# A gated delta rule among projection products: the silu clamp on another engine, scan steps at other distances, and one product with ones

## The chip, the cores and the metric

The kernel runs on one core of one Trainium2 chip. The metric is the device time of one execution in microseconds, the median of several runs. A core has five engines that work side by side and wait for each other through semaphores: TensorE (PE in the profile, its weight loads PEld), VectorE (DVE), ScalarE (ACT), GpSimd (POOL) and SyncE (SP, which issues most of the DMAs here). Each engine takes its own instructions in a fixed order.

## The reference

The trunk has two layers, each with a mixer and a SwiGLU channel mixer, and ends with a modulated RMSNorm. It is applied to two groups, 512 and 256 tokens wide, with shared weights. The kernel keeps both side by side, 768 tokens, with features on the 128 partitions. The first layer mixes with a Fourier transform. The second is the bidirectional gated delta rule with 8 heads of width 128, and all of the change lies in it:

```python
def gdn_mixer(h, w_in, conv_w, a_log, dt_bias, norm_g, w_out):
    proj = h @ w_in
    qkv = silu(centred_depthwise_conv(proj[..., :GDN_QKV_DIM], conv_w))     # 5 taps
    z = ...; ab = ...                                                       # the rest of proj
    q = l2norm(q) * (GDN_HEAD_DIM ** -0.5)
    k = l2norm(k)
    g = -exp(a_log) * softplus(ab[:, :, 0:2] + dt_bias)
    beta = sigmoid(ab[:, :, 2:4])
    o_fwd = gated_delta_chunked(q, k, v, g[:, :, 0], beta[:, :, 0])
    o_bwd = gated_delta_chunked(q[:, ::-1], k[:, ::-1], v[:, ::-1], ...)[:, ::-1]
    o = o_fwd + o_bwd
    o = o * rsqrt(mean(o * o) + EPS) * norm_g * silu(z)
    return o @ w_out
...
    # gated_delta_chunked, per chunk: a triangular system, then a scan over the chunks
    sol = triangular_solve(I + strict(kb @ k.T * decay), [v * beta, kb * exp(gc)])
    def step(state, xs):
        delta = u_i - w_i @ state
        o = qd_i @ state + qk_i @ delta
        state = state * gl_i + kd_i.T @ delta
```

## The kernel before

**The whole.** First the Fourier layer with its channel mixer, then the delta stage, then the second channel mixer and the final norm. Large products are done in three passes with operands split into a high and a low part (hh and hl for the activations, wh and wl for the weights; `split_w`, lines 147 to 153, casts on ScalarE and subtracts on DVE).

**A head.** `prepare` (line 811) runs for the 8 heads in turn. It makes four projection products, for k, q, v and z, each over 8 chunks of the input features for the 512-token segment and then for the 256-token segment, 3 passes each, so 48 matmuls a product (`product`, line 188). k, q and v go through `conv_block` (line 756): ScalarE evicts the product into `pad` and a scaled copy into `wa`, DVE adds four taps to it (line 768), and then comes a silu. It is made from exponentials so that ScalarE keeps one table: `silu_factor` (line 712) clamps its input at -44 on GpSimd (line 713) and does Exp, Ln with bias 1 and Exp on ScalarE (lines 714 to 716); DVE multiplies the factor in (lines 772, 773). z gets the same factor (line 866).

**Placed steps.** Beside its products a head has smaller steps, which are placed among the products by a plan written out by hand. After each chunk of a product `tick` (line 732) adds 0.421 x 3 x its width to a counter `now`, which is 647 for a 512-wide chunk and 323 for a 256-wide one; 7760 for a product and 31040 for a head. Whatever is due by then is traced at that place, inside `issue_after`, which ties its TensorE instructions behind the chunk's last matmul (`run_next`, line 727). A step of the other engines is not tied, and a scheduler that orders each engine's queue by its own estimate of when an instruction is ready has the last word, so a step can stand later than its place. `PLACES` (line 57) gives five places counted from the head's start: the norm of k, the k-by-k product and the solver (`chunk_kk`, which also stores the matrix to DRAM for it), the decayed q, the k-by-q product, and the transposed v. `SCAN` (line 58) is where the scan of the head begins. `HOPS` (line 56) has the distances between the steps of the scan.

**The solver** (line 870) inverts the 16 by 16 diagonal blocks: the matrix goes to DRAM (`atd`) and comes back as lanes (`uu`), some 30 small DVE operations follow, and the result goes by DRAM (`solved`) into `cc`. GpSimd prepares the masked matrix `am` (line 897).

**The scan** (lines 899 and 946) first builds the full inverse in three levels of 16, 32 and 64. At a level, in the names used below, T are the transposes of `cc` (line 915; masked by DVE at line 917), Z the product with `am` (copied out by ScalarE at line 929), and R the product that updates `cc` on DVE (line 939) or, at level 64, is copied into `rr` by ScalarE (lines 942, 943). So T16 needs the solver's `cc`, and R64 needs the copy of Z64. Distances: HOPS[0] ahead of T32 and T64, HOPS[1] from T to Z, HOPS[2] from Z to R. Then come four steps over the token chunks, in both directions at once: pk (the state with k; DVE makes `xx`, line 975), py (`xx` with `rr`; ScalarE makes `yk` and `yy`), pu (`yk` with k; DVE makes the state `st`, line 992), at distances HOPS[3], [4] and [5]. The first step has no pk and the last no pu; the steps are numbered 0 to 3. After HOPS[6] the output products follow (lines 995 to 1006), and after HOPS[7] the norm: ones times the squares of q, and ones times the squares of the output, summed in PSUM (lines 1017, 1018), then Ln and Exp on ScalarE and two products on DVE; the result goes to DRAM (`ogd`), for the last head straight into hh and hl.

**Order of heads.** The scan of a head starts in the next head's products. After the last head all that is due for head 6 is run at once (line 1032), the results are loaded back from `ogd`, and seven output products over heads 0 to 6 carry the scan of head 7. Most buffers of the scan exist once (`rr`, `yy`, `xx`, `am`, `st`), those of a head twice (`kT`, `qd`, `pm`, `cc`, `zs`), and three PSUM banks `sm` serve all of the scan's products.

Of the kernel before, what the change touches and what calls it, by code (L numbers as in the profile page):

```python
# [15 lines left out]
ALU = mybir.AluOpType  # L16
# [36 lines left out]
LANES = NT * P // BASE  # L53
LSTEP = BASE * (P + 1)
NEGBIG = -1e30
HOPS = (1150.0, 1080.0, 1150.0, 1130.0, 830.0, 2080.0, 1150.0, 720.0)
PLACES = (16100.0, 20200.0, 22900.0, 29400.0, 36200.0)
SCAN = 35100.0

_TAB = {}  # L60

# [48 lines left out]
def encoder_kernel(  # L110
# [5 lines left out]
    V, A_, G = nc.vector, nc.scalar, nc.gpsimd  # L116
# [7 lines left out]
    ones = const.tile([P, P], F32, name="ones")  # L124
# [6 lines left out]
    def mm(out, lhsT, rhs, start=True, stop=True, **kw):  # L131
        return nc.tensor.matmul(out, lhsT, rhs, start=start, stop=stop, **kw)  # L132
# [31 lines left out]
    def load_block(w2d, k0, kc, m0):  # L164
        stg = fetch(w2d, k0, kc, m0)
        ah, al = [], []
        step = kc if kc <= HK else (kc + 1) // 2
        for a in range(0, kc, step):
            n = min(step, kc - a)
            wh, wl = split_w(stg[:, a : a + n])  # L170
            ah += [wh[:, k] for k in range(n)]
            al += [wl[:, k] for k in range(n)]
        return ah, al
# [14 lines left out]
    def product(pool, w, ah, al, kc, tick=None):  # L188
        out = []
        for g, (lo, ln) in enumerate(SEGS):  # L190
            ps = bank(pool, g)[:, :ln]
            for last in passes(ps, w, [a[:, lo : lo + ln] for a in ah[:kc]], [a[:, lo : lo + ln] for a in al[:kc]]):
                if tick:
                    tick(ln * 3 * 0.421, last)
            out.append(ps)
        return out
# [283 lines left out]
    with ExitStack() as l0:  # L480
# [8 lines left out]
        with ExitStack() as fs:  # L489
# [41 lines left out]
            for c in range(KC):  # L531
                pcs.append(fp.tile([P, NC + NS], F32, name="xt", bufs=8))
                ps = pbig.tile([P, 1024], F32, name="big")
                oc, os_ = 0, 512
                for g, s in ((0, S0), (1, S1)):
                    for par in (0, 1):
# [3 lines left out]
                        for kt in range(nkt):  # L540
                            o, n = COLS[f"seq{g}_{kt}_{par}"]
                            src = (odd if par else even)[2 if g else kt][:, c * P : (c + 1) * P]
# [71 lines left out]
    with ExitStack() as gs:  # L614
# [16 lines left out]
        def work(name="wa", bufs=2):  # L631
            return ga.tile([P, T + 2], F32, name=name, bufs=bufs)
# [76 lines left out]
        o16 = COLS["eye16"][0] - FCOLS  # L709
        eye16 = gtab[:LANES, o16 : o16 + BASE * BASE]  # L710

        def silu_factor(e, src, eng):
            eng.tensor_scalar(e, src, -44.0, None, ALU.max)  # L713
            A_.activation(e, e, AF.Exp, scale=-1.0)  # L714
            A_.activation(e, e, AF.Ln, bias=1.0)
            A_.activation(e, e, AF.Exp, scale=-1.0)
# [39 lines left out]
        def conv_block(h, which, pool, tag, bufs):  # L756
            wb = load_block(win, 0, KC, which * D + h * P)
            pq = product(ppr, wb, hh, hl, KC, tick)
            wc = [cwT[:, d * 24 + which * 8 + h : d * 24 + which * 8 + h + 1] for d in range(5)]
            acc = work()  # L760
            with tc.high_priority():
                A_.copy(pad[:, 2 : 2 + S0], pq[0])
                A_.copy(pad[:, S0 + 4 : T + 4], pq[1])
                A_.activation(acc[:, :S0], pq[0], AF.Copy, scale=wc[2])
                A_.activation(acc[:, S0 + 2 :], pq[1], AF.Copy, scale=wc[2])  # L765
            G.memset(acc[:, S0 : S0 + 2], 0.0)
            for d in (0, 1, 3, 4):
                V.scalar_tensor_tensor(acc, pad[:, d : d + T + 2], wc[d], acc, ALU.mult, ALU.add)  # L768
            e = work("we")
            silu_factor(e, acc, G)  # L770
            out = pool.tile(head_shape, F32, name=tag, bufs=bufs)
            V.tensor_tensor(out[:, :S0], acc[:, :S0], e[:, :S0], ALU.mult)
            V.tensor_tensor(out[:, S0:], acc[:, S0 + 2 :], e[:, S0 + 2 :], ALU.mult)
            return out
# [33 lines left out]
        def both(ap, n=NT):  # L808
            return ap.unsqueeze(1).to_broadcast([P, 2, n, P])

        def prepare(h):
            def col(t, d, j):
                return t[:, j, d * 8 + h : d * 8 + h + 1]

            raw = raws[h]
            base = line["now"]
            kT = conv_block(h, 1, gp, "kT", 2)
            qd = gp.tile([P, 2, NT, P], F32, name="qd", bufs=2)
            A_.activation(qd, raw, AF.Exp)
            pm = gp.tile([P, 2, NT, P], F32, name="pm", bufs=2)  # L820
            for d in range(2):
                G.affine_select(pm[:, d], raw[:, d], pattern=[[0, NT], [1 - 2 * d, P]], compare_op=ALU.is_ge, fill=NEGBIG,
                                base=0, channel_multiplier=2 * d - 1)
                for j in range(NT):
                    A_.activation(pm[:, d, j], pm[:, d, j], AF.Exp, bias=col(ngml, d, j))
            at = gp.tile([P, NT, P], F32, name="at", bufs=2)
            V.tensor_tensor(at, pm[:, 0], pm[:, 1], ALU.add)
            out = {"pm": pm, "qd": qd, "at": at, "kT": kT}

            def norm_k():  # L830
                rs = feat_norm(kT, work()[:, :T], work("we")[:, :T])
                V.tensor_tensor(kT, kT, rs, ALU.mult)

            def chunk_kk():
                pairwise(kT, kT, lambda b0, ps: V.tensor_tensor(at[:, b0 : b0 + NB], ps, at[:, b0 : b0 + NB], ALU.mult))
                atd = dgp.tile([NT * UN], F32, name="atd")
                nc.sync.dma_start(dram_full(atd), at)
                out["cc"] = solve(h, atd)
                siblings(out, LEVELS[0])
                out["kk"] = token_major(kT, "kk")  # L840

            def decay_q():
                V.tensor_tensor(qd, qd, both(tiles6(qT)), ALU.mult)

            def chunk_kq():
                pairwise(kT, qT, lambda b0, ps: V.tensor_tensor(pm[:, :, b0 : b0 + NB], both(ps, NB), pm[:, :, b0 : b0 + NB], ALU.mult))

            def values():
                out["vk"] = token_major(vT, "vk")

            for t, fn in zip(PLACES, (norm_k, chunk_kk, decay_q, chunk_kq, values)):
                at_time(base + t, fn)
            at_time(base + SCAN, run(scan(h, out)))
            qT = conv_block(h, 0, ga, "qT", 2)
            out["qT"] = qT
            if h < H - 1:
                raws.append(fetch_gc(h + 1))
            vT = conv_block(h, 2, ga, "vT", 1)
            wb = load_block(win, 0, KC, 3 * D + h * P)
            pz = product(ppr, wb, hh, hl, KC, tick)  # L860
            e = work("we")[:, :T]
            zs = gp.tile([P, T], F32, name="zs", bufs=2)
            with tc.high_priority():
                for g, (lo, ln) in enumerate(SEGS):
                    A_.copy(zs[:, lo : lo + ln], pz[g])
            silu_factor(e, zs, G)
            V.tensor_tensor(zs, e, zs, ALU.mult)
            out["zs"] = zs

# [29 lines left out]
        def invert(src):  # L899
# [4 lines left out]
            for lv in LEVELS:  # L904
# [4 lines left out]
                if lv != LEVELS[0]:  # L909
                    yield HOPS[0]  # L910
                t1 = {}
# [6 lines left out]
                if lv == LEVELS[-1]:  # L918
                    for d in range(2):
                        G.affine_select(rr[:, d], cc, pattern=[[0, NT], [1 - 2 * d, P]], compare_op=ALU.is_ge, fill=0.0,  # L920
                                        base=0, channel_multiplier=2 * d - 1)
                yield HOPS[1]
                zz = {}
# [6 lines left out]
                if lv != LEVELS[-1]:  # L930
                    siblings(src, 2 * lv)
                yield HOPS[2]
                for b0 in halves:
# [12 lines left out]
        def scan(h, src):  # L946
# [5 lines left out]
            vk, zs = src["vk"], src["zs"]  # L952
# [5 lines left out]
            for stp in range(4):  # L958
# [11 lines left out]
                if stp:  # L970
                    yield HOPS[3]
                    pk = group(lambda d, j: kT[:, j * P : (j + 1) * P], lambda i: st[:, first - 4 + i], len(live))
# [4 lines left out]
                else:  # L977
                    xin = lambda i: vk[:, live[i][1]]
                yield HOPS[4]
                py = group(lambda d, j: rr[:, d, j], xin, len(live))  # L980
# [4 lines left out]
                if more:  # L985
                    yield HOPS[5]
                    pu = group(lambda d, j: kk[:, j], lambda i: yk[:, i], more)
# [21 lines left out]
            sq = gp.tile([P, 2 * NT, P], F32, name="yy")  # L1009
            so, sq = sq[:, :NT].rearrange(flat), sq[:, NT:].rearrange(flat)  # L1010
            A_.activation(sq, src["qT"], AF.Square, scale=P * math.sqrt(EPS))
            A_.activation(so, ob, AF.Square)
            yield HOPS[7]
            rs = gp.tile([P, 2, NT, P], F32, name="rr")[:, 0].rearrange(flat)
            for lo, ln in SEGS:
                ps = psm.tile([P, 512], F32, name="sm")
                mm(ps[:, :ln], ones, sq[:, lo : lo + ln], stop=False)
                mm(ps[:, :ln], ones, so[:, lo : lo + ln], start=False)
                A_.activation(rs[:, lo : lo + ln], ps[:, :ln], AF.Ln, bias=epsq, scale=1.0 / P)
            A_.activation(rs, rs, AF.Exp, scale=-0.5)  # L1020
            V.scalar_tensor_tensor(ob, ob, gT[:, 48:49], rs, ALU.mult, ALU.mult)
# [148 lines left out]
```

## Time and profile before

| | us |
|---|---|
| median of 3 runs | 1996.56 (1994.72 to 2004.65) |
| the profiled execution | 2001.88 |
| its span, first to last instruction | 2000.10 |
| PE busy in the span | 1877.7 |
| DVE busy | 1229.2 |
| ACT busy | 894.4 |
| POOL busy | 468.0 |
| delta stage, from k of head 0 to the last output product | about 770 to 1410 |

The profile is one execution. Its rows give an instruction's engine, line, operation and tiles (out<-in), with start and length in us; a square bracket at the end gives the idle time ahead of it and who ended it. Waits are put down to the instruction that came last by semaphore, which is not always the one that was really late. Most matmuls have line 132, since one helper issues them; they are told apart by their tiles. A matmul's length in a row is its latency: the next one starts before it ends, so the spacing of starts is what it holds the engine for. An f32 product counts as two passes in the rows.

### The profile page before, as it was taken

How to read it: one execution, taken by the hardware profiler on the slowest of the kernel's cores; microseconds unless marked ns; L12 is line 12 of the kernel's file. 1: busy time of each engine (PE TensorE's matmuls, PEld its weight loads, DVE VectorE, ACT ScalarE, POOL GpSimd, SP SyncE). 2: the span in 40 equal slices, each digit the busy share in tenths (PEclk: the TensorE clock that was granted, in tenths of full speed). 3: DMA queues.
4: the chain of work that ended last, by engine and by line, in shares of the span. 5: the costliest groups of instructions: out<-in, count | busy, mean ns of one | idle time of the engine just before them, and what ended most of it. 6: DMA issues, size and time to landing. Idle time of an engine off the chain costs nothing.

```text
span 2000.1 us, 29707 instructions
## 1 busy us (share of the span) xinstructions
PE 1877.7 (94%) x11529; PEld 1657.3 (83%) x11529; DVE 1229.2 (61%) x2009; ACT 894.4 (45%) x1712; POOL 468.0 (23%) x370
## 2 busy tenths in 40 slices
PE   8898999999999999889898898889789999999998
PEld 6585989989798987778777777778579998999998
DVE  4637645545454657877686677664685565656565
ACT  3525524424142446655655656543454352524243
POOL 1314202111111101243333332320341211111231
PEclk9999999999999999999999999989889999999999
DMA  7654234453533144211121221141122222222211
GB/s 261 212 179 137 77 108 138 132 185 118 183 116 117 55 130 125 73 48 49 54 74 41 62 66 47 50 144 38 51 55 57 74 70 64 69 78 74 62 55 64
DMA packets 250662, 189.71 MB, mean 95 GB/s; under 512 B 20624, under 2 KB 219417, under 8 KB 250521
## 3 DMA queue, kind: packets, MB, share of 16 engines
q1 hardware_dynamic: 250112, 187.66, 31.1%
q8 instruction: 90, 1.47, 0.3%
q14 instruction: 51, 0.42, 0.1%
q10 hardware_dynamic: 409, 0.15, 0.0%
HBM read 174.36 MB, written 13.42 MB: 94 GB/s over the span
## 4 chain that ended last, share of the span: by engine, by line
PE 71%; DVE 10%; DMA 5%; POOL 5%; ACT 4%; issue 4%; SPq 0%; DVEq 0%; POOLq 0%; ACTq 0%
PE pr L132 60%; PE sm L132 9%; POOL we L713 3%; DVE wa L768 3%; DVE wl L152 1%; DMA cc<-solved 1%; DMA at<-in_ada_w_dram 1%; ACT we L714 1%; DVE g L349 1%; PE big L132 1%; PE ax L132 1%; DMA stg<-in_ffn_w_gu_dram 1%; ACT wh L151 1%; DMA xt<-in_x_prompt_dram 1%; DVE r L908 0%
## 5 line engine op out<-in xcount | busy, mean ns | idle before, releaser
L151 ACT CAST wh<-stg 128x512 fp32r<-128x512 f32 (+1 forms) x468 | 278.4, 597 | 623.9 <-PE pr L132 566.6
L132 PE MATMUL pr<-hh,wh 128*128 128x384 f32 (+2 forms) x1488 | 520.7, 352 | 20.3 <-ACT sg L403 7.3
L132 PE MATMUL pr<-hl,wh 128*128 128x384 f32 (+2 forms) x1488 | 510.4, 343 | 7.8 <-DVE hl L200 6.4
L132 PE MATMUL pr<-hh,wl 128*128 128x384 f32 (+2 forms) x1488 | 510.8, 343 | 0.9 <-DVE wl L152 0.9
L152 DVE TENSOR_TENSOR wl<-stg,wh 128x512 fp32r<-128x512 f32 (+1 forms) x468 | 348.4, 746 | 230.9 <-ACT wh L151 220.6
L132 PEld LDWEIGHTS pr<-hh,wh 128*128 128x128 f32 x1488 | 283.4, 191 | 48.4 <-ACT sg L403 9.0
L132 PE MATMUL pr<-g,wh 128*128 128x512 f32 (+1 forms) x1280 | 317.7, 339 | 0.0
L132 PEld LDWEIGHTS pr<-hl,wh 128*128 128x128 f32 x1488 | 284.3, 191 | 24.7 <-DVE hl L200 8.0
L132 PEld LDWEIGHTS pr<-hh,wl 128*128 128x128 f32 x1488 | 284.0, 191 | 17.8 <-DVE wl L152 1.7
L132 PEld LDWEIGHTS pr<-g,wh 128*128 128x128 f32 x1280 | 217.3, 188 | 38.8 <-issue 6.2
L132 PE MATMUL pr<-g,wl 128*128 128x512 f32 (+1 forms) x640 | 215.2, 337 | 0.0
L379 POOL TENSOR_TENSOR s<-stg 128x512 f32<-128x512 f32 x44 | 61.5, 1398 | 647.8 <-DMA stg<-in_ffn_w_gu_dram 548.7
L132 PE MATMUL pr<-el,wh 128*128 128x384 f32 x528 | 180.9, 343 | 4.3 <-POOL el L200 4.3
L132 PE MATMUL pr<-eh,wh 128*128 128x384 f32 x528 | 181.0, 344 | 3.7 <-ACT eh L199 3.7
L132 PE MATMUL pr<-eh,wl 128*128 128x384 f32 x528 | 179.6, 340 | 0.0
L454 DVE SCALAR_TENSOR_TENSOR x<-pr,modT,x 128x512 f32<-128x512 f32 x96 | 59.0, 616 | 125.7 <-PE pr L132 125.4
L132 PEld LDWEIGHTS pr<-g,wl 128*128 128x128 f32 x640 | 120.2, 188 | 14.5
L443 POOL TENSOR_TENSOR up<-m,up 128x384 f32<-128x384 f32 x44 | 52.9, 1203 | 283.2 <-ACT up L403 283.2
L132 PEld LDWEIGHTS pr<-eh,wh 128*128 128x128 f32 x528 | 100.4, 190 | 10.1 <-ACT eh L199 4.3
L132 PEld LDWEIGHTS pr<-el,wh 128*128 128x128 f32 x528 | 100.7, 191 | 7.1 <-POOL el L200 6.8
L768 DVE SCALAR_TENSOR_TENSOR wa<-pad,cwT,wa 128x770 f32<-128x770 f32 x96 | 99.8, 1040 | 4.9 <-ACT wa L765 3.4
L132 PEld LDWEIGHTS pr<-eh,wl 128*128 128x128 f32 x528 | 100.8, 191 | 0.0
(342 smaller groups left out, 2776.3 us busy)
## 6 DMA issues: line engine op xcount, KB each, us to landing
stg<-in_ffn_w_gu_dram SPq DMA_DIRECT2D x88, 512.0 KB, 4.4
at<-in_ada_w_dram SPq DMA_DIRECT2D x112, 256.0 KB, 3.6
at<-in_ada_w_dram SPq DMA_DIRECT2D x40, 512.0 KB, 4.8
stg<-in_gdn_w_in_dram SPq DMA_DIRECT2D x33, 512.0 KB, 4.1
stg<-in_ffn_w_down_dram SPq DMA_DIRECT2D x48, 256.0 KB, 2.9
stg<-in_ffn_w_down_dram SPq DMA_DIRECT2D x32, 320.0 KB, 3.2
at<-in_final_ada_w_dram SPq DMA_DIRECT2D x32, 256.0 KB, 3.9
raw<-gcd SPq DMA_DIRECT2D x8, 768.0 KB, 4.7
```

The costliest lines, as they stand in the source:

```text
L132: return nc.tensor.matmul(out, lhsT, rhs, start=start, stop=stop, **kw)
L151: A_.copy(wh[:, :n], src)
L152: V.tensor_tensor(wl[:, :n], src, wh[:, :n].bitcast(F32), ALU.subtract)
L349: (G if m in YP else V).tensor_tensor(t, xs[m], rs, ALU.mult)
L379: eng.tensor_tensor(out, a, b, op)
L443: G.tensor_tensor(up[i][:, HT:], m7[i], up[i][:, HT:], ALU.add)
L454: V.scalar_tensor_tensor(x[:, lo : lo + ln], ps[g], modT[:, gate, m, g : g + 1], x[:, lo : lo + ln], ALU.mult, ALU.add)
L713: eng.tensor_scalar(e, src, -44.0, None, ALU.max)
L714: A_.activation(e, e, AF.Exp, scale=-1.0)
L768: V.scalar_tensor_tensor(acc, pad[:, d : d + T + 2], wc[d], acc, ALU.mult, ALU.add)
```

## The change

Three things change, all in the delta stage. The clamp of each silu goes from GpSimd to DVE (three convolution blocks and z, in each of 8 heads). In the norm at the end of a scan GpSimd adds the squares of q to the squares of the output, and one product with ones per segment takes the place of two. And the plan's distances change: HOPS[1] from 1080 to 1300, HOPS[2] from 1150 to 1500, HOPS[3] from 1130 to 1400, HOPS[4] from 830 to 1300, HOPS[7] from 720 to 2700, while a scan starts at 34100 instead of 35100. `PLACES` stays.

```diff
-HOPS = (1150.0, 1080.0, 1150.0, 1130.0, 830.0, 2080.0, 1150.0, 720.0)
+HOPS = (1150.0, 1300.0, 1500.0, 1400.0, 1300.0, 2080.0, 1150.0, 2700.0)
 PLACES = (16100.0, 20200.0, 22900.0, 29400.0, 36200.0)
-SCAN = 35100.0
+SCAN = 34100.0
...
-        def silu_factor(e, src, eng):
-            eng.tensor_scalar(e, src, -44.0, None, ALU.max)
+        def silu_factor(e, src):
+            V.tensor_scalar(e, src, -44.0, None, ALU.max)
...
-            silu_factor(e, acc, G)
+            silu_factor(e, acc)
...
-            silu_factor(e, zs, G)
+            silu_factor(e, zs)
...
             A_.activation(so, ob, AF.Square)
+            G.tensor_tensor(so, so, sq, ALU.add)
             yield HOPS[7]
             rs = gp.tile([P, 2, NT, P], F32, name="rr")[:, 0].rearrange(flat)
             for lo, ln in SEGS:
                 ps = psm.tile([P, 512], F32, name="sm")
-                mm(ps[:, :ln], ones, sq[:, lo : lo + ln], stop=False)
-                mm(ps[:, :ln], ones, so[:, lo : lo + ln], start=False)
+                mm(ps[:, :ln], ones, so[:, lo : lo + ln])
```

## The prediction

> **What bounds the kernel now.** I read the page's head and its chain first, then the windows by head, then TensorE's waits in the delta stage, then the timeline of one head.
>
> ```profile
> span 2000.1 us, 29707 instructions
> PE 1877.7 (94%) x11529; PEld 1657.3 (83%) x11529; DVE 1229.2 (61%) x2009; ACT 894.4 (45%) x1712; POOL 468.0 (23%) x370
> PE pr L132 60%; PE sm L132 9%; POOL we L713 3%; DVE wa L768 3%; DVE wl L152 1%; DMA cc<-solved 1%; DMA at<-in_ada_w_dram 1%; ACT we L714 1%; DVE g L349 1%; PE big L132 1%; PE ax L132 1%; DMA stg<-in_ffn_w_gu_dram 1%; ACT wh L151 1%; DMA xt<-in_x_prompt_dram 1%; DVE r L908 0%
> ```
>
> TensorE is busy 94% of the span and most of the chain is its products; but the chain also has 3% "POOL we L713", the clamp that the change moves, and only the delta stage runs that line. The windows cut this stage into heads (columns: stretch and its length, busy time of PE, PEld, DVE, ACT and POOL, then the granted clock).
>
> ```profile
> 786.00:860.00 74.00, 66.08 (x400) 56.78 (x400) 59.61 (x100) 48.26 (x95) 23.36 (x19) 0.98 0.30 80
> 955.00:1028.00 73.00, 64.96 (x428) 56.44 (x427) 51.59 (x95) 42.04 (x87) 25.39 (x17) 1.00 0.21 58
> 1028.00:1101.60 73.60, 66.24 (x427) 57.71 (x426) 51.60 (x95) 41.68 (x85) 25.36 (x17) 0.98 0.21 57
> 1174.40:1248.00 73.60, 66.28 (x428) 57.67 (x427) 51.58 (x95) 41.76 (x86) 25.02 (x16) 0.98 0.21 56
> ```
>
> A head takes 73.0 to 74.0 us and TensorE stands still for 7.3 to 8.0 us of it (73.60 less 66.28, 73.00 less 64.96). TensorE is the bound, with a tenth of each head lost in waits; DVE is at 70%. The waits of TensorE between 770 and 1410 us are these (who waited for whom, total us, times, longest):
>
> ```profile
> PE sm L132 <- ACT t L929: 13.1, 6, 2.3
> PE sm L132 <- ACT we L714: 7.9, 5, 1.6
> PE ax L132 <- DVE kT L832: 6.9, 6, 1.6
> PE sm L915 <- DMA cc<-solved: 6.2, 6, 1.2
> PE sm L132 <- DVE t L917: 5.7, 8, 0.8
> PE pr L132 <- ACT hh L199: 4.1, 2, 3.2
> PE sm L132 <- DVE st L992: 3.4, 5, 0.7
> PE ax L798 <- DVE vT L772: 3.3, 1, 3.3
> PE sm L132 <- DVE xx L975: 2.7, 2, 1.9
> ```
>
> These nine hold 53.3 us, five to eight times the same wait, one for each head. The timeline of one head shows how the largest comes about:
>
> ```profile
> 1192.19 2.51 POOL L897 TENSOR_TENSOR am<-at,gtab 128x768 f32<-128x768 f32 x1 [4.38 <-PE sm L132]
> 1194.67 2.44 POOL L713 TENSOR_SCALAR we<-wa 128x770 f32<-128x770 f32 x1
> 1197.14 0.85 ACT L714 ACTIVATE we<-we 128x770 f32<-128x770 f32 x1 [4.58 <-POOL we L713]
> 1201.59 0.84 ACT L929 COPY t<-sm 128x384 f32<-128x384 f32 x2
> 1202.11 1.94 PE L132 MATMUL sm<-r,t 128*128 128x128 f32 x12 [2.29 <-ACT t L929]
> ```
>
> GpSimd does the mask product of the inversion (am) first, then the clamp of k's silu. ScalarE idles 4.58 us for that clamp, then works through the silu, the evictions and the square of k in order, and only then copies out the inversion's product (L929). The last product of the 64 level (R64) waits 2.29 us for this copy. The wait is made by the clamp's place, not by the inversion.
>
> **The change part by part.** The clamps first. 24 clamps of 770 columns and 8 of 768 leave GpSimd for DVE.
>
> ```profile
> L713 POOL TENSOR_SCALAR we<-wa 128x770 f32<-128x770 f32 x24 | 53.1, 2214 | 90.9 <-DVE wa L768 41.0 <-DVE tmp L885 28.6 <-DVE rl L886 14.1
> L512 DVE TENSOR_SCALAR odd<-xt,ss 128x1024 f32<-128x1024 f32 x3 | 2.2, 745 | 0.0
> L768 DVE SCALAR_TENSOR_TENSOR wa<-pad,cwT,wa 128x770 f32<-128x770 f32 x96 | 99.8, 1040 | 4.9 <-ACT wa L765 3.4
> ```
>
> The nearest row for the new form is L512, the same operation kind on 1024 columns: 0.745 us, or 0.56 us scaled down to 770. The convolution's L768, same width but two inputs, is the upper bound, 1.04 us. I take 0.65 us, near L512. So the silu starts at least 2.21 - 0.65 = 1.6 us sooner after the convolution; for k, where GpSimd was still busy with am, 2.48 us more (1194.67 less 1192.19). That is 4 us, more than the 2.29 us for which R64 waited. DVE carries 4 x 0.65 = 2.6 us more per head, 51.6 to 54.2 us of about 69, under other work: TensorE waits for a DVE result only where a step stands close behind it. If that cover is gone it costs 4 x 1.04 = 4.2 us per head.
>
> R64's wait: 13.1 us, all gone, **-13.1**. Behind it hangs the clock:
>
> ```profile
> 1199.60:1202.10 2.50, 0.21 (x2) 0.00 (x1) 1.03 (x2) 2.47 (x6) 0.11 (x1) 1.00 0.00 0
> 1204.00:1206.00 2.00, 2.00 (x10) 1.81 (x9) 0.20 (x1) 1.45 (x4) 0.00 (x0) 0.50 0.00 0
> ```
>
> Two us after that idle stretch the granted clock is 0.50. By the head rows above it falls in some heads (0.98, a loss of 0.02 x 73.6 = 1.5 us) and not in others (1.00). Three of the heads quoted show it: **-4.5**; the bounds are 0, if another wait keeps dropping the clock, and 12, if all 8 heads paid 1.5 us. [...]
>
> Next the spacing. A step's delay is in units of the plan, in which one projection product counts 7760; its steps are only tied behind that place, and may stand later. Worked out on the grid of 647 (512-wide) and 323 (256-wide), with the places in head h+1 of head h's scan: first transposes T16 from k, first segment, chunk 6, to chunk 4; R64 from q, second segment, chunk 5, to v, first segment, chunk 1; last-but-one step py3 from z, second segment, chunk 6, to the next head's k, second segment, chunk 0; the output products from k chunk 1 of head h+2 to its second segment, chunk 4; the norm from its k chunk 3 to q chunk 2. So the tail of scan h now runs among the first steps of scan h+1.
>
> The wait put down to L714 (7.9 us) is at py3, whose xx is really late on DVE:
>
> ```profile
> 1237.17 0.94 DVE L846 TENSOR_TENSOR pm<-ax,pm 128x768 f32<-128x768 f32 x1
> 1238.04 0.67 DVE L152 TENSOR_TENSOR wl<-stg,wh 128x512 fp32r<-128x512 f32 x1
> 1238.84 0.33 DVE L975 SCALAR_TENSOR_TENSOR xx<-sm,neg,vk 128x128 f32<-128x128 f32 x1
> 1239.32 0.46 PE L132 MATMUL sm<-xx,rr 128*128 128x128 f32 x2 [1.59 <-ACT we L714]
> ```
>
> xx stands behind the mask products of k and q (L846) and a weight split. After the change py3 is not among them and has 1300 instead of 830 units: **-7.9**. The k norm (L832) loses the clamps of k and q ahead of it on ScalarE; of 6.9 us I take **-5**. Of the other step waits on DVE (5.7 + 3.4 + 2.7 = 11.8) I take half, since wider steps help but DVE is fuller: **-6**.
>
> The sum of squares of q and the output goes from two products with ones to one, with an add on GpSimd before it:
>
> ```profile
> 1246.99 2.85 PE L132 MATMUL sm<-yy,ones 128*128 128x512 f32 x8
> 1249.49 0.58 PE L132 MATMUL pr<-hl,wh 128*128 128x512 f32 x1
> ```
>
> The pair holds TensorE from 1246.99 to 1249.49, 2.50 us; half goes, 1.25 us in 8 heads: **-10.0**. The add has the shape of am in the row above, 2.51 us on GpSimd, which gave up 4 x 2.2 us. Behind it in GpSimd's queue stand am, the r2 masks and the selects; the one who waits for it is the norm's product, 2700 instead of 720 units later, so it costs nothing there.
>
> Two losses. First, T16 waits 1.2 us for the solved blocks already; it is planned two chunks sooner, and the clamps of v and z stand on DVE among the solver's steps, 2 x 0.65 us. Half of this is made good by the k norm being sooner; 0.65 us in 7 heads, **+5**; it could be -6 (that wait goes as well) or far more (third rival). Second, when the last z product ends, scan 6 still has pu2, pk3, py3, output and norm to do, where before it had the last two, and the output projection needs head 6 (the 4.1 us on L199 are this wait). Three more steps of 0.33 (xx) and 0.46 us (its product) and the add, 3 x 0.8 + 2.5 = 4.9, less what T16 of scan 7 fills in: **+4**, between 0 and 8. Scan 7 ends a product and more later among the seven output products, still ahead of the eighth, which needs it: 0.
>
> Sum: -13.1 - 4.5 - 7.9 - 5 - 6 - 10.0 + 5 + 4 = -37.5 us. The profiled execution took 2001.88 us with its span of 2000.10; it becomes 1964.4. The median of the three runs is 5.3 us lower, 1996.56, so the median becomes **1959**. The terms' bounds give 1945 to 1972 for this case.
>
> **The rivals.** *All of it goes.* Wider steps and a free GpSimd remove the nine waits whole: -53.3 - 4.5 - 10.0 = -67.8, 1929. For it: each wait is under 3.3 us and wider steps are worth more than that. Against: the hh and cc waits hang on DMAs that nothing here shortens. Chance 0.10.
>
> *DVE becomes the bound.* What DVE pays while GpSimd works is seen in these rows:
>
> ```profile
> 1236.05 2.35 POOL L713 TENSOR_SCALAR we<-zs 128x768 f32<-128x768 f32 x1 [4.13 <-ACT zs L865]
> 1236.34 0.90 DVE L886 TENSOR_TENSOR rl<-rl,tmp 48x126 f32<-48x126 f32 x1
> 1239.87 0.28 DVE L886 TENSOR_TENSOR rl<-rl,tmp 48x126 f32<-48x126 f32 x1
> ```
>
> The same instruction takes 0.90 us beside a GpSimd clamp and 0.28 us without. If each clamp on DVE meets a GpSimd operation and stands for its whole 2.51 us, DVE has 51.6 + 4 x (1.04 + 2.51) = 65.8 us in a head of 69 and no slack; the terms 7.9, 5 and 6 stay as they are. Left are -13.1 - 4.5 - 10.0 + 5 + 4 = -18.6, or 1978. [...] Against it: GpSimd is busy only 25 of 73 us, 9 of them the clamps that go, and the clamps' own contention goes with them. Chance 0.17.
>
> *T16 waits for the solver: slower.* The rows are a product standing alone, part of the output's passes, and T16:
>
> ```profile
> 91.48 8.59 PE pr L132 x48
> 1242.58 1.06 PE L132 MATMUL sm<-pm,yy 128*128 128x128 f32 x8
> 1177.79 0.28 PE L132 MATMUL pr<-hh,wh 128*128 128x256 f32 x1
> 1179.30 0.85 PE L915 MATMUL sm<-ident,cc 128*128 128x128 f32 x6 [1.23 <-DMA cc<-solved]
> ```
>
> If T16 stands at its planned place, TensorE gets there earlier by two 512-wide chunks (two thirds of 8.59 us are eight such chunks: 1.4 us), by the norm's 2.5 us and by the 40 output passes of 0.13 us, 5.3 us, which now come after it; the solver is 1.3 us later by the two clamps. That is 10.5 us a head, 73.5 us in seven, against 42.5 us of gain without the +5: slower by 31 us, 2028. It decides from 42.5/7 = 6.1 us a head. Against it, in the trace of before T16 stands after the seventh 256-wide pass, in chunk 2 of the second segment, and not at its plan's chunk 6 of the first: the order in TensorE's queue follows an estimate of readiness beside the plan. The next steps follow T16 wherever it stands. Chance 0.10.
>
> *The spacing does nothing.* Steps that are tied to a place may stand later anyway; the waits reappear on other releasers, and only the product with ones pays: -10.0 + 4 = -6, 1991. Chance 0.08.
>
> **How the numbers follow.** The forecast has 0.55. A measurement of this kernel can tell about 0.5%, 10 us, from no change. Faster by more: the forecast, the first rival and three quarters of the second, 0.77; within: the spacing rival and the rest, 0.13; slower: the third rival, 0.10. The range 1932 to 1991 leaves out the third rival, half of the first and the edges of the others, about 0.2.
>
> **What would show it.** Right: no L713 on POOL, L713 on DVE at 0.55 to 0.7 us; no wait of sm on ACT t L929, and ScalarE's idle ahead of L714 below 1 us; heads of 68 to 69 us; half as many sm<-yy,ones; clock 1.00 in every head. Wrong: L713 near 2 us or more on DVE with DVE above 60 us a head (second rival); sm L915 waiting over 6 us a head on cc (third); PE idle still 7 us a head with other names (fourth).

## The result, and the profile after

The changed kernel takes 1953.14 us (median of 4 runs, 1951.27 to 1956.79) against 1999.95 us of the kernel before (median of 4, 1994.72 to 2004.65). The ratio is 0.9772 [0.9756, 0.9789], or 46 us faster by the ratio (the two medians are 46.8 us apart). The forecast was 1959 us, a gain of 37.5 us.

The head of the page of the changed kernel and its chain. Its profiled execution took 1951.27 us:

```profile
span 1949.5 us, 29608 instructions
PE 1850.7 (95%) x11497; PEld 1635.5 (84%) x11497; DVE 1242.4 (64%) x2041; ACT 891.5 (46%) x1712; POOL 403.8 (21%) x346
PE pr L132 62%; PE sm L132 8%; DVE wa L768 2%; DVE wl L152 1%; PE ax L132 1%; DMA at<-in_ada_w_dram 1%; DMA cc<-solved 1%; DVE g L349 1%; POOL yy L1013 1%; ACT wh L151 1%; DVE we L713 1%; DMA stg<-in_ffn_w_gu_dram 1%; PE big L132 1%; DVE tmp L885 1%; ACT we L714 1%
```

"POOL we L713" has left the chain, and GpSimd is busy 64 us less. Two names of changed lines are new there, with 1% each: the clamp on DVE, and GpSimd's add "POOL yy L1013". Now the window of the delta stage, first of the kernel before, then of the changed one:

```profile
771.00:1406.00 635.00, 576.58 (x3676) 499.61 (x3675) 436.02 (x805) 348.87 (x706) 195.59 (x136) 0.98 0.24 66
```

```profile
768.00:1358.00 590.00, 554.46 (x3645) 481.97 (x3644) 450.58 (x837) 345.95 (x706) 132.52 (x112) 1.00 0.26 71
```

The delta stage goes from 635 to 590 us. What lies ahead of it went from 771 to 768 us and what lies behind it from 594.1 to 591.5, with no change in the program there; that much is put down to the difference of two executions. Of the stage's 45 us, about half is idle time of TensorE (635.00 less 576.58 is 58.4 us, 590.00 less 554.46 is 35.5 us) and half its busy time (576.58 to 554.46, 22.1 us less). Ten of those 22 are put down to the halved product with ones (8 x 1.25 us); the other 12 agree with the clock, granted at 0.98 before and at 1.00 now: 0.02 x 635 = 12.7 us.

TensorE's waits in the changed kernel, 770 to 1370 us, the longest of them (one of 1.2 us on L454, ahead of the last row, and those below 1.1 us are left out):

```profile
PE sm L132 <- POOL yy L1013: 7.1, 6, 1.3
PE sm L915 <- DMA cc<-solved: 5.4, 5, 1.6
PE sm L915 <- DVE cc L939: 4.7, 6, 1.2
PE sm L132 <- POOL wa L766: 3.4, 2, 1.7
PE sm L132 <- DVE xx L975: 2.8, 2, 1.9
PE sm L132 <- ACT rr L943: 2.0, 6, 0.6
PE sm L132 <- DVE t L917: 1.9, 4, 0.5
PE sm L132 <- DVE st L992: 1.4, 1, 1.4
PE ax L132 <- DVE kT L832: 1.1, 2, 0.7
```

ACT t L929 (13.1 us), ACT we L714 (7.9) and ACT hh L199 (4.1) are gone, and kT L832 is down from 6.9 to 1.1. The largest wait is one that did not exist before: the product with ones stands for GpSimd's add. The rows put down to L766, a memset of 0.10 us behind the add in GpSimd's queue, are the same wait. This is how it looks in two heads:

```profile
961.14 1.56 PE L132 MATMUL sm<-yy,ones 128*128 128x512 f32 x4 [1.35 <-POOL yy L1013]
1036.17 1.56 PE L132 MATMUL sm<-yy,ones 128*128 128x512 f32 x4 [1.69 <-POOL wa L766]
```

A row of the pair took 2.85 us, one product takes 1.56. What is saved goes again into the idle time ahead of it.

The groups of the changed lines and of two beside them:

```profile
L768 DVE SCALAR_TENSOR_TENSOR wa<-pad,cwT,wa 128x770 f32<-128x770 f32 x96 | 109.9, 1145 | 4.8 <-ACT wa L765 3.6
L714 ACT ACTIVATE we<-we 128x770 f32<-128x770 f32 x24 | 20.4, 851 | 15.2 <-DVE we L713 15.2
L713 DVE TENSOR_SCALAR we<-wa 128x770 f32<-128x770 f32 x24 | 18.6, 775 | 0.4
L1013 POOL TENSOR_TENSOR yy<-yy 128x768 f32<-128x768 f32 x8 | 14.5, 1815 | 66.3 <-ACT yy L1012 66.3
```

ScalarE's idle time ahead of L714 is 15.2 us in 24, 0.63 us a time, as forecast below 1 us. The clamp is 0.775 us on average where 0.65 was taken, and the convolution's tap L768 rose from 1.040 to 1.145 us; the section on the hardware says why.

Last, the stage cut into heads 2 to 6 and the end (from the DMA of head 7's matrix to the first weight of the channel mixer), before and after:

```profile
927.61:1293.54 365.93, 328.55 (x2138) 286.39 (x2136) 255.27 (x475) 209.57 (x427) 124.17 (x84) 0.99 0.20 55
1293.54:1406.47 112.93, 106.05 (x646) 91.58 (x644) 60.09 (x115) 41.97 (x82) 19.24 (x10) 0.94 0.30 89
```

```profile
916.67:1255.74 339.07, 318.19 (x2123) 278.09 (x2122) 268.21 (x498) 207.38 (x426) 83.91 (x69) 1.00 0.23 62
1255.74:1358.38 102.64, 96.39 (x635) 84.33 (x634) 59.22 (x118) 41.17 (x80) 16.12 (x10) 1.00 0.31 92
```

A head went from 73.2 (365.93 / 5) to 67.8 us, the forecast's 68 to 69. The end, for which a loss of 4 us was forecast, gained 10.3 us, and its clock went from 0.94 to 1.00.

### The profile page after: what moved, and what is told of

It reads as the page before. It is cut to its first block, busy times and chain, and to the rows that moved or that the text cites. A ratio compares the mean times of both kernels' runs of the same rounds, so it can differ in the third digit from the quotient of the medians.

```text
span 1949.5 us, 29608 instructions
## 1 busy us (share of the span) xinstructions
PE 1850.7 (95%) x11497; PEld 1635.5 (84%) x11497; DVE 1242.4 (64%) x2041; ACT 891.5 (46%) x1712; POOL 403.8 (21%) x346
## 4 chain that ended last, share of the span: by engine, by line
PE 72%; DVE 12%; ACT 6%; DMA 5%; POOL 3%; issue 2%; SPq 0%; DVEq 0%; ACTq 0%; POOLq 0%
PE pr L132 62%; PE sm L132 8%; DVE wa L768 2%; DVE wl L152 1%; PE ax L132 1%; DMA at<-in_ada_w_dram 1%; DMA cc<-solved 1%; DVE g L349 1%; POOL yy L1013 1%; ACT wh L151 1%; DVE we L713 1%; DMA stg<-in_ffn_w_gu_dram 1%; PE big L132 1%; DVE tmp L885 1%; ACT we L714 1%
## 5 line engine op out<-in xcount | busy, mean ns | idle before, releaser
L132 PE MATMUL pr<-hh,wh 128*128 128x384 f32 (+2 forms) x1488 | 512.8, 347 | 14.9 <-ACT sg L403 6.2
L454 DVE SCALAR_TENSOR_TENSOR x<-pr,modT,x 128x512 f32<-128x512 f32 x96 | 58.9, 616 | 126.7 <-PE pr L132 126.3
L768 DVE SCALAR_TENSOR_TENSOR wa<-pad,cwT,wa 128x770 f32<-128x770 f32 x96 | 109.9, 1145 | 4.8 <-ACT wa L765 3.6
```

Of the source, the lines that this page charges most:

```text
L454: V.scalar_tensor_tensor(x[:, lo : lo + ln], ps[g], modT[:, gate, m, g : g + 1], x[:, lo : lo + ln], ALU.mult, ALU.add)
```

## The experiments

The theory at the start was the forecast's: the clamp's place makes the waits, the spacing adds to that, the products are a matter of the one step. The first four kernels do the parts alone and two together; their times are against 1997.19 us, the median of the kernel before on that chip.

**The clamp alone.** Everything else as before.

```diff
-            silu_factor(e, acc, G)
+            silu_factor(e, acc, V)
...
-            silu_factor(e, zs, G)
+            silu_factor(e, zs, V)
```

> Clamps on DVE alone, old distances, two products with ones. Theory (the clamp's place made the largest waits): ACT's idle ahead of L714 falls below 1 us a time, R64's 13.1 us wait on ACT t L929 goes and so does half of the k norm's, 18 to 25 us faster. Rival (the waits come from steps standing too close, whatever the clamp): under 6 us faster, since R64 then waits for something else.

Measured: 1966.75 us, 0.9844 [0.9823, 0.9866], 31 us faster; more than the theory's upper end, far from the rival. Three of the rows of TensorE's waits:

```profile
PE sm L132 <- DVE t L917: 9.7, 9, 2.0
PE pr L132 <- ACT hh L199: 6.5, 2, 4.7
PE ax L132 <- DVE kT L832: 0.9, 3, 0.3
```

L929 and L714 are no longer in the list and the k norm's wait is nearly gone: 13.1 + 7.9 + 6.0 us, of which t L917 takes back 4.0 and hh 2.4; 20.6 us are left. The clock can explain what the theory's upper end lacks: it is at 0.50 for 3.4 us of the stage, where before it was for 27.3, which can be 12 us. It is 1.00 in heads 2 to 6, and a head takes 68.0 us, nearly the 67.8 of the changed kernel. So the clamp's place did make the waits, py3's among them, for which the prediction wanted the spacing.

**The spacing alone.** The clamp stays on GpSimd, the product a pair.

```diff
-HOPS = (1150.0, 1080.0, 1150.0, 1130.0, 830.0, 2080.0, 1150.0, 720.0)
+HOPS = (1150.0, 1300.0, 1500.0, 1400.0, 1300.0, 2080.0, 1150.0, 720.0)
-SCAN = 35100.0
+SCAN = 34100.0
```

> Distances HOPS[1] to [4] and SCAN of the changed kernel alone; clamps stay on GpSimd, two products with ones, HOPS[7] stays 720. Theory: py3's 7.9 us and half of the other step waits go, about 10 to 14 us faster, and ScalarE still idles some 3 to 4 us for each k clamp. Rival (spacing does nearly all): 25 us or more. Third theory (T16 waits for the solver): slower, with sm L915 waiting over 6 us a head on cc.

Measured: 1985.61 us, 0.9938 [0.9918, 0.9958], 12 us faster, as the theory had it.

Three of the rows of TensorE's waits:

```profile
PE sm L915 <- DMA cc<-solved: 14.2, 7, 3.0
PE sm L132 <- ACT yy L1011: 5.5, 6, 2.7
PE sm L132 <- ACT t L929: 1.6, 1, 1.6
```

R64's wait is gone here too, by distance. But T16 waits 14.2 us instead of 6.2 for the solver, and new waits stand for ScalarE's ob L1006 (7.5 us) and its squares L1011 (5.5). This is the third rival's mechanism, at 1.1 us a head where that rival priced 10.5. Heads take 71.7 us, 1.5 less than before; the end is 105.6 instead of 112.9.

**The one product alone**, with its longer distance and the add.

```diff
             A_.activation(so, ob, AF.Square)
+            G.tensor_tensor(so, so, sq, ALU.add)
             yield HOPS[7]
...
-                mm(ps[:, :ln], ones, sq[:, lo : lo + ln], stop=False)
-                mm(ps[:, :ln], ones, so[:, lo : lo + ln], start=False)
+                mm(ps[:, :ln], ones, so[:, lo : lo + ln])
```

> One product with ones behind GpSimd's add, HOPS[7] at 2700, nothing else changed. By the prediction's step: 10 us faster, since the add costs nothing at its later place. Rival, from the changed kernel's profile, where sm waits 7.1 us on POOL yy L1013 and 3.4 us more at the same place: the add's wait takes it all back, within 3 us of before, the wait on L1013 being 0.8 us or more a head.

Measured: 1999.93 us, 1.0013 [0.9999, 1.0027]. The prediction's step of 10 us brings nothing; its rival here, no gain, is right.

```profile
PE sm L132 <- POOL yy L1013: 4.5, 4, 1.3
PE sm L132 <- POOL wa L766: 4.2, 4, 1.1
```

8.7 us of waiting (770 to 1410 us) stand at this product. The order of the steps shifts as well: t L917 waits 13.3 us instead of 5.7, ACT t L929 6.8 instead of 13.1.

**Clamp and spacing**, the changed kernel less the one product (the pair and HOPS[7] as before).

```diff
-HOPS = (1150.0, 1300.0, 1500.0, 1400.0, 1300.0, 2080.0, 1150.0, 2700.0)
+HOPS = (1150.0, 1300.0, 1500.0, 1400.0, 1300.0, 2080.0, 1150.0, 720.0)
...
-            G.tensor_tensor(so, so, sq, ALU.add)
...
-                mm(ps[:, :ln], ones, so[:, lo : lo + ln])
+                mm(ps[:, :ln], ones, sq[:, lo : lo + ln], stop=False)
+                mm(ps[:, :ln], ones, so[:, lo : lo + ln], start=False)
```

> Clamps on DVE and the new distances, but two products with ones and HOPS[7] at 720. If the one product pays its 10 us, this is 36 us faster than before against the changed kernel's 46; if the add's wait eats it, it is as fast as the changed kernel within 4 us, 42 to 50 us faster than before.

Measured: 1952.85 us, 0.9776 [0.9755, 0.9796], the changed kernel's time. 31 and 12 us add up to 43, and 45 are measured: the two add up, and the third part is worth nothing. From head 2 to the end:

```profile
915.60:1250.20 334.60, 322.04 (x2129) 281.85 (x2129) 263.70 (x496) 206.30 (x423) 74.04 (x64) 1.00 0.23 62
1250.20:1355.38 105.18, 102.61 (x664) 90.69 (x663) 56.89 (x120) 43.10 (x84) 11.57 (x8) 0.98 0.31 93
```

Over both rows TensorE is busy 424.65 us and idle 15.1 us. In the changed kernel (318.19 + 96.39) it is busy 414.58 and idle 27.1. What the product saves in busy time (10.1 us, of which the clock of the end, 0.98 against 1.00, can be 2) comes back as 12.0 us of idle time.

The next four, against 1998.73 us, ask how the add's wait can be avoided, what a clamp on DVE costs, and what the earlier scan does.

**The norm later.** The changed kernel, with the norm's product 1600 units further from the add in heads 0 to 5.

```diff
-            yield HOPS[7]
+            yield HOPS[7] + (1600.0 if h < H - 2 else 0.0)
```

> The changed kernel with the norm's product tied 1600 units later (HOPS[7] 2700 becomes 4300 in heads 0 to 5). Theory (the one product pays nothing because TensorE stands 0.8 to 1.7 us a head for GpSimd's add): the 10.5 us of waits on yy L1013 and wa L766 at this product go, 6 to 10 us faster than the changed kernel, 52 to 56 us faster than before. Rival (TensorE would have stood somewhere else anyway; DVE and ScalarE set the head's length by now): within 3 us of the changed kernel.

Measured: 1950.10 us, 0.9760 [0.9739, 0.9782], 2.4 us under the changed kernel's ratio, within the intervals; the rival had that, and the theory, which had 6 to 10 us, missed. The wait at the product falls from 10.5 to 4.3 us, and the steps that it now stands among wait more (t L917 1.9 to 5.5, xx L975 2.8 to 4.0). The distance is a lower bound on the place, and a later place takes another step's time.

**The add on DVE.** The changed kernel, with the add on the other engine.

```diff
-            G.tensor_tensor(so, so, sq, ALU.add)
+            V.tensor_tensor(so, so, sq, ALU.add)
```

> The changed kernel with the add of the squares on DVE instead of GpSimd. Theory (the add's own 1.8 us on GpSimd is what the product waits for): an add of about 0.95 us on DVE halves the wait, 4 to 6 us faster than the changed kernel. Rival (DVE is as full as it can be, so that its 0.95 us come back as other waits): same or slower than the changed kernel.

Measured: 1947.82 us, 0.9748 [0.9728, 0.9767], 4.8 us under the changed kernel's ratio (0.0024 x 1998.73), as the theory had it, though the two intervals overlap.

```profile
L1013 DVE TENSOR_TENSOR yy<-yy 128x768 f32<-128x768 f32 x8 | 7.6, 953 | 7.1 <-ACT yy L1012 7.1
```

The add takes 0.953 us instead of 1.815 and no product with ones waits for it. About half of the 10 us are had this way, as far as the intervals tell.

**The clamp twice.** Clamp and spacing, with each clamp made twice on DVE (the second gives the same values).

```diff
             eng.tensor_scalar(e, src, -44.0, None, ALU.max)
+            eng.tensor_scalar(e, src, -44.0, None, ALU.max)
```

> Clamps on DVE and the new distances with two products with ones (the fourth run), each clamp now done twice on DVE. Theory (the clamps' 0.6 us lie under other work): 32 more of them are 20 us more on DVE, and the time rises by under 6 us. Rival (DVE is the bound): 15 to 25 us slower than the fourth run, that is only 20 to 30 us faster than before.

Measured: 1961.34 us, 0.9812 [0.9792, 0.9832], 7 us slower than clamp and spacing. That fits neither theory. The delta stage of this kernel (the columns as before):

```profile
770.00:1364.40 594.40, 564.03 (x3660) 490.92 (x3659) 464.19 (x866) 346.80 (x703) 114.38 (x102) 1.00 0.25 70
```

DVE is busy 464.19 us in it, against 442.85 with one clamp each (770.00 to 1355.38 us). A third of these 21 us shows in the time, and the second clamp also makes each silu later. So a clamp on DVE is not free, where the prediction's sum put it at nothing, but it is mostly hidden.

**The scan where it was.** Clamp and spacing, with the scan's start as before.

```diff
-SCAN = 34100.0
+SCAN = 35100.0
```

> The fourth run with SCAN back at 35100. Theory (T16 stands where its input is estimated ready, not at its planned place): within 3 us of the fourth run. Rival (an earlier T16 makes TensorE wait for the solver): 5 us or more faster than the fourth run, and the waits of sm L915 on DMA cc fall from 4.3 us to below 2.

Measured: 1964.50 us, 0.9829 [0.9811, 0.9848], 10.6 us slower than with 34100. Both theories missed: neither expected that the earlier start pays so much. The heads take 68.0 us (with 34100 66.9), the end 114.7 us (105.2). In the two profiled executions that is 15 us; other parts of the program are some 3 us shorter in this one. Two of TensorE's waits, and rows at the end:

```profile
PE sm L915 <- DVE cc L939: 8.9, 6, 1.5
PE sm L132 <- ACT yy L1011: 8.2, 6, 1.7
```

```profile
1286.63 2.85 PE L132 MATMUL sm<-yy,ones 128*128 128x512 f32 x8
1300.27 1.01 PE L132 MATMUL pr<-hh,wh 128*128 128x512 f32 x2 [3.97 <-ACT hh L199]
1302.28 1.48 PE L915 MATMUL sm<-ident,cc 128*128 128x128 f32 x6
```

The later start does what the prediction expected of it at T16 (the wait for cc from the solver falls from 4.3 to 0.8), but the waits for cc L939 and for the squares L1011 grow by 10.3 us together (from 6.0 and 0.8), and at the end head 6's output comes 13.6 us behind its norm's product, with nothing to do for the last 4. T16 of head 7, which needs none of it, stands behind that.

The last four are against 1998.37 us.

**The late start, early in head 7 alone.** On the kernel just measured:

```diff
-            at_time(base + SCAN, run(scan(h, out)))
+            at_time(base + SCAN - (1000.0 if h == H - 1 else 0.0), run(scan(h, out)))
```

> Clamps on DVE and the new distances, two products with ones; SCAN is 35100 in heads 0 to 6 and 34100 in head 7 alone. Theory (the earlier SCAN pays only at the end, where T16 of head 7 is tied ahead of the output product that stands for head 6): 7 to 10 us faster than with 35100 in all heads, back to within 4 us of 34100 in all. Rival (it pays in each head): within 3 us of 35100 in all heads.

Measured: 1959.20 us, 0.9800 [0.9778, 0.9822]. About half of the 10.6 us comes back, which is less than the one theory and more than the other had. The wait for hh is gone, because this now stands ahead of it:

```profile
1290.35 0.81 PE L915 MATMUL sm<-ident,cc 128*128 128x128 f32 x6
1291.69 0.83 PE L132 MATMUL sm<-t,am 128*128 128x128 f32 x6
```

By the profiled executions, what is left lies in the heads (67.9 against 66.9 us) and at the end (109.2 against 105.2); heads 0 and 1 and the parts outside the stage give back some of it. Still there are the waits for cc L939 (9.1) and L1011 (6.7).

**The same edit on the kernel before**, as a test whether the end's gain can be had without the rest.

```diff
-            at_time(base + SCAN, run(scan(h, out)))
+            at_time(base + SCAN - (1000.0 if h == H - 1 else 0.0), run(scan(h, out)))
```

> The kernel before with one edit: SCAN 34100 in head 7 alone. Theory (as in the run before): TensorE's wait of 3.2 us on hh L199 and the slow clock behind it go, 5 to 9 us faster than before. Rival (the gain at the end needs the other edits): within 3 us of before.

Measured: 1997.55 us, 0.9998 [0.9984, 1.0012]. The theory missed, its rival holds.

```profile
1321.74 2.85 PE L132 MATMUL sm<-yy,ones 128*128 128x512 f32 x8
1328.62 0.82 PE L915 MATMUL sm<-ident,cc 128*128 128x128 f32 x6
1337.02 1.43 PE L132 MATMUL pr<-hh,wh 128*128 128x512 f32 x3 [4.08 <-ACT hh L199]
1339.11 1.98 PE L132 MATMUL sm<-t,am 128*128 128x128 f32 x12
```

T16 of head 7 has gone ahead of the wait, but the next step (Z16, the product of t with am) stands behind it, and the wait for hh is only longer. The DMA that brings cc of head 7 is issued 1.6 us behind the norm's product of head 6 in the changed kernel (1284.9 and 1283.30) and 1.8 us here (1323.6 and 1321.74), so that does not look like what differs; why Z16 comes ahead of the wait in the one and not in the other was not settled.

**py's distances alone.** The kernel before, with py and pu moved back.

```diff
-HOPS = (1150.0, 1080.0, 1150.0, 1130.0, 830.0, 2080.0, 1150.0, 720.0)
+HOPS = (1150.0, 1080.0, 1150.0, 1400.0, 1300.0, 2080.0, 1150.0, 720.0)
```

> The kernel before with HOPS[3] at 1400 and HOPS[4] at 1300, nothing else. By the prediction's step py3's wait of 7.9 us goes with the distance: 5 to 8 us faster. Rival (the distances only move the place from which a step may start, and the wait turns up at another step): within 3 us of before, with the waits of sm on xx L975 and ACT we L714 under 3 us but others longer.

Measured: 1990.77 us, 0.9955 [0.9939, 0.9971], 9 us faster, a little over the theory's 5 to 8. Three of the rows of TensorE's waits:

```profile
PE sm L132 <- DVE xx L975: 8.6, 14, 1.9
PE sm L132 <- ACT yy L1011: 8.1, 5, 2.1
PE sm L132 <- ACT t L929: 1.6, 1, 1.6
```

L714 is out of the list, and of L929's 13.1 us 1.6 are left although R64's own distance is as before. Other waits take part of it, as the rival had it: xx L975 8.6 us instead of 2.7, yk L983 6.5, and hh 7.2 instead of 4.1. So the large waits were a matter of the whole order and not of one distance: they go by the clamp alone, by the spacing alone, and mostly by py's distances alone.

**A better version.** The changed kernel with the add on DVE, and the scan at 35100 except in head 7 (34100).

```diff
-SCAN = 34100.0
+SCAN = 35100.0
...
-            at_time(base + SCAN, run(scan(h, out)))
+            at_time(base + SCAN - (1000.0 if h == H - 1 else 0.0), run(scan(h, out)))
...
-            G.tensor_tensor(so, so, sq, ALU.add)
+            V.tensor_tensor(so, so, sq, ALU.add)
```

> The changed kernel with the add of the squares on DVE, and SCAN 35100 in heads 0 to 6, 34100 in head 7. Theory (an earlier SCAN costs TensorE the 6.2 us of waits for cc that the run with the add on DVE still has): 2 to 5 us faster than that run, 53 to 56 us faster than before. Rival (T16 stands where cc is estimated ready, whatever SCAN): within 2 us of that run.

Measured: 1942.72 us, 0.9727 [0.9705, 0.9749], faster than both kernels and 4 us below the add on DVE alone, within the theory's 2 to 5, though the intervals overlap.

```profile
918.12:1242.89 324.77, 311.31 (x2093) 274.42 (x2091) 261.94 (x497) 204.17 (x423) 72.86 (x64) 1.00 0.22 62
```

A head takes 65.0 us and TensorE stands still for 2.7 us of it (324.77 less 311.31, by 5), where it was 7.5 before and 4.2 in the changed kernel. With the pair of products these two starts cost 5 us (0.9800 against 0.9776), here none is seen; whether their price depends on the norm is not shown, since the intervals overlap in both pairs.

## Why the prediction was right, and where it was not

**The mechanism** holds. The clamp on GpSimd held up ScalarE and with it the inversion's copy; the clamp alone brings 31 of the 46 us. Put against the waits of the stage, term by term (us; measured is the change of the wait by name, unless said):

| step of the prediction | forecast | measured |
|---|---|---|
| R64's wait, ACT t L929 | -13.1 | -13.1 |
| the clock behind it | -4.5 | about -12, the rest of the fall in busy time |
| py3, ACT we L714 | -7.9 | -7.9 |
| the k norm, DVE kT L832 | -5 | -5.8 |
| other step waits (t L917, st L992, xx L975: 11.8 to 6.1) | -6 | -5.7 |
| one product for two | -10.0 | -10 in busy time, +10.5 in waits |
| T16 and what follows it (cc 6.2 to 5.4, cc L939 1.9 to 4.7, rr L943 0.5 to 2.0) | +5 | +3.5 |
| the end, ACT hh L199 | +4 | -4.1 |
| sum | -37.5 | -44.6 |

The stage went down by 45.0 us. The sum is no test of its own, since the clock's 12 us are what was left over of the busy time, and smaller waits are not in the table (vT L772 fell by 2.2 us, for one).

That the forecast came so near is in part luck. The one product was too good by 10.5 us; the clock and the end were put too low by 7.5 and 8.1, and between them they more than made up for it. The bounds were not added up from the terms either: those that the prediction names (the clock 0 to 12, T16 down to -6, the end 0 to 8) give 1937 to 1968, where it says 1945 to 1972. And not all of its nine waits stand once in each head: hh, xx and vT stand once or twice.

**The clock was the term sized too small.** In the traces the granted clock falls to 0.50 for 3.41 us at a time, or for a multiple of that. In the stage of the kernel before it was there for 27.3 us: 3.41 us in each of four heads and 6.83 us twice at the end. In the changed kernel it never was. Half of 27.3 is 13.7 us, the most that this can be worth. Only three heads were counted, at 1.5 us each; the fourth (from 1274.91) and the end (0.94 over 112.93 us is 6.8 us) were not.

The fall was rightly read from the trace, behind a wait of 2.29 us. But the length of the wait alone does not decide it. Here is the stretch ahead of that fall, and two stretches of the head before it (columns as in the windows above: TensorE's busy time stands first, the granted clock third from the end):

```profile
1199.82:1203.23 3.41, 1.12 (x10) 1.13 (x11) 1.24 (x3) 3.19 (x7) 0.00 (x0) 1.00 0.00 0
1124.70:1128.11 3.41, 2.12 (x19) 1.92 (x17) 1.03 (x2) 3.31 (x6) 1.99 (x3) 1.00 0.00 0
1128.11:1131.53 3.42, 2.44 (x20) 2.40 (x21) 0.69 (x1) 3.17 (x9) 0.00 (x0) 1.00 0.00 0
```

In the first TensorE is idle for 2.29 of 3.41 us, and the clock is at 0.50 in the next 3.41, to 1206.64. In the other two the same wait (2.27 us, ahead of 1129.09) lies across the border, with 1.29 us idle on one side and 0.98 on the other, and no fall follows. The falls of one trace lie whole multiples of 3.41 us apart. Cut on that grid, between 760 and 1350 us of all 14 traces, 30 of 30 stretches with at least 1.88 us idle were followed by one at 0.50, 7 of 36 with 1.50 to 1.88, and 8 of 2353 with less, seven of these 8 already at 0.50. So in these traces a wait cost clock or not by where it fell, which the prediction could not know. That the changed kernel has no fall is in part luck too: its longest wait is 1.9 us, and so is that of clamp and spacing, which has one fall at the end, behind 1.59 us idle:

```profile
1265.94:1269.35 3.41, 1.82 (x8) 0.83 (x6) 3.41 (x10) 2.05 (x5) 0.00 (x0) 1.00 0.66 195
1269.35:1272.76 3.41, 3.03 (x11) 2.76 (x12) 3.23 (x9) 1.59 (x3) 0.00 (x0) 0.50 0.85 287
```

**The step that failed is the one product**, in the sentence that the norm's product comes "2700 instead of 720 units later, so it costs nothing there". The distance bounds the place from below in the plan's units, but it does not make a wait impossible: the add starts only when ScalarE's second square is done (66.3 us of idle time ahead of L1013, all of it ended by L1012), lasts 1.8 us, and the product stands in TensorE's queue ahead of it being done. What was saved came back one for one. The product alone showed 0, clamp and spacing without it the changed kernel's time, and the add on DVE 5 us. No run has one product at the old distance, so what the longer distance costs by itself is not known.

**The sign at the end was wrong.** The prediction saw scan 6's longer tail and "what T16 of scan 7 fills in" as the smaller part. The earlier start of scan 7 was the larger part: in the changed kernel T16, Z16 and R16 of head 7 (1289.24 to 1294.77) stand where head 6's output is on its way, between its norm's product (1283.30) and its cast to hh (1294.69), and the wait for hh is gone. Starting the scan later brought it back (3.97 us at one place), and starting only head 7 early took it away again. It is not the whole of the 10.3 us: the clamp alone, with the old start, has an end of 107.9 us, and there it can be the clock, which is at 0.50 for 3.4 us instead of 13.7.

**T16** came out near the forecast in its number and not in its mechanism: the wait for the solver fell by 0.8 us, and those for the updates of cc behind R16 and R32 grew (cc L939). And py3's wait, for which the prediction took the distance, went by the clamp alone as well as by the distance alone; what the row was really late for was not taken apart.

**The rivals.** All goes: it did not; 35.5 us of idle time are left. DVE becomes the bound: DVE is busy 53.6 us in a head of 67.8 (268.21 / 5), and what a clamp pays beside GpSimd is real, but 8 of 32 paid it (last section). Doubling the clamps cost 7 us, so the cover holds mostly. T16 waits for the solver: it is seen in the spacing alone, at a tenth of its price, and it decides nothing. The spacing does nothing: it brought 12 us alone.

**Open.** Why the scan at 35100 costs 5 us beyond head 7's part, with the pair of products, is only narrowed down: the squares (L1011) and the updates of cc come later. ScalarE's idle time ahead of L714 is 58.6 us there (11.6 with 34100), and the squares stand behind L714 in its queue, which fits, but no run took this apart.

## What to carry to other kernels

An elementwise step between two stages of another engine is worth a trial on the engine that does it fastest and has room at that time; here 2.2 us on GpSimd became 0.78 on DVE. What it costs is read from who is queued behind its consumer, not from its own length. Work that is taken off the bounding engine can come back as a wait if a slower engine must first prepare it, as here (10 us off TensorE's busy time, 10.5 us of waits for an add of 1.8 us on GpSimd): look for when the prepared operand is ready. And where the tail of one loop has a gap, the next one's first steps, if they are independent, can be worth more there than their own waits.

## What the runs showed of the hardware

The clamp on DVE has two prices. These are a row of GpSimd and three of DVE in the changed kernel:

```profile
1025.08 2.65 POOL L897 TENSOR_TENSOR am<-at,gtab 128x768 f32<-128x768 f32 x1 [2.75 <-PE sm L132]
```

```profile
967.69 2.47 DVE L768 SCALAR_TENSOR_TENSOR wa<-pad,cwT,wa 128x770 f32<-128x770 f32 x1
1013.82 0.56 DVE L713 TENSOR_SCALAR we<-wa 128x770 f32<-128x770 f32 x1
1026.09 2.06 DVE L713 TENSOR_SCALAR we<-wa 128x770 f32<-128x770 f32 x1
```

With GpSimd quiet it takes 0.54 to 0.57 us. The clamp at 1026.09 starts while am runs and ends at 1028.15, which is 0.42 us after am has ended (1027.73). Nine of the 32 clamps started while a GpSimd operation ran. Eight of them end 0.41 to 0.42 us after that operation; the ninth, at 856.01, started 0.04 us behind an L920 on GpSimd and took 0.54 us. The other 23 take 0.54 to 0.57 us, among them three during which am started. So in eight of nine cases a clamp that started beside a GpSimd operation was done only 0.4 us after its end, three quarters of its own length. The mean of 0.775 us is that of short clamps with a few such meetings in it. A tap of the convolution, 1.01 us alone in most rows, was 2.47 us beside another am. All 16 of the 96 taps that started while a GpSimd operation ran took 1.50 to 2.55 us, the other 80 took 1.01 us on average; in the kernel before it was 3 of 96 (1.50 to 2.61 us). It was the prediction's second rival, and it met a quarter of the clamps and a sixth of the taps; GpSimd is busy 16.8 us of a head (83.91 / 5) once the clamps are gone from it.
